# A pooling shift row computed in column tiles, a narrower band, and modulation rows paced anew with a third buffer

## The chip, the cores and the metric

The kernel runs on one core of a Trainium2 chip. The metric is the device time of one execution in microseconds, the median of three runs. Beside the runs there is one profiled execution, from which all rows of the trace come. Engines are named as the profile names them: PE is TensorE (PEld its weight loads), DVE VectorE, ACT ScalarE, POOL GpSimd, SP SyncE, which issues most of the transfers. A name with a q behind it (SPq, ACTq) is the engine's queue of transfers.

## What is computed

Two small transformer stacks in sequence over one sequence of 256 tokens and 1024 features, in float32. The first stack is an mLSTM and sparse-attention layer and then a gated recurrent layer (HGRN2). The second has two layers, each of a mixer and an MLP, both modulated by a vector computed from a conditioning input `c`:

```python
def modulate(h, shift, scale):
    return h * (1.0 + scale[:, None, :]) + shift[:, None, :]

c_act = jax.nn.silu(c)
for i in range(DEPTH):                       # DEPTH = 2
    mod = c_act @ ada_w[i] + ada_b[i]        # 1024 x 6144 weights for each layer
    sh1, sc1, g1, sh2, sc2, g2 = jnp.split(mod, 6, axis=-1)
    h = modulate(rmsnorm(x, norm_mix_g[i]), sh1, sc1)
    y = pool_mixer(h, ...) if i == 0 else sgu_mixer(h, ...)
    x = x + g1[:, None, :] * y
    h = modulate(rmsnorm(x, norm_mlp_g[i]), sh2, sc2)
    x = x + g2[:, None, :] * sq_relu_mlp(h, mlp_w1[i], mlp_w2[i])
return rmsnorm(x, final_g)
```

`pool_mixer` splits the features into four groups of 256. In each it takes the mean over the last 2, 4, 8 or 16 tokens less the token itself, and multiplies by a 256 x 256 matrix. `sq_relu_mlp` is `square(relu(h @ w1)) @ w2` with 4096 hidden features.

## The kernel before, in words

Activations lie transposed, features on the 128 partitions and 256 tokens on the free axis, in eight tiles `xT[:, k, :]`. A float32 product is made of three products in a reduced float32 format: both operands are split into a high and a low part (`hi`, `lo`), and high-high, low-high and high-low are summed (lines 216 to 223). Weights come in pieces of 128 x 1024 (512 KB), two to a load of 1 MB (`load_raw`, line 150; three buffers `raw`). ScalarE copies a piece to `whi` and VectorE subtracts it into `wlo` (lines 155 to 163; four buffers each). The first product of an MLP has 32 tiles of 24 matmuls, one piece each; the second has 8 output tiles of 4 pieces with 16 matmuls each (lines 1002 to 1049).

**Modulation.** The generator `ada` (line 338) computes the two vectors `mod` of 48 columns. For each of 96 chunks it loads 128 x 1024 weights (512 KB, tile `araw`, two buffers, line 350), and VectorE multiplies them with the row `crow` and sums along the row into one column (line 351). This is no work for TensorE. The generator pauses after every one or two chunks; 6 pauses make 8 chunks. `step(upto)` (line 360) runs it to its next pause, as far as `upto` sixths have not been reached, and `finish(upto)` (line 367) runs it up to there. Calls of `step` are spread over all layers: in the first layers up to 30 steps, then one before every second tile of the first MLP's first product (line 1011), one before every second piece of its second (line 1030), one before each tile of the gated layer until 66 steps are done (line 1079), and then one before every fourth tile of the second MLP's first product (line 1013).

**Order.** The order of instructions on each engine is fixed when the program is built, by a list scheduler that goes by the written order as a priority, takes what is ready, and lowers the priority of what `step` issues a little (line 364). What is written late can therefore stand early, if buffers and engine are free. At run time each engine keeps this order, SP's queue of transfers too.

**Pooling** (`pool_layer`, line 960) multiplies by the matrix first, then by a band matrix that does the moving means. Tiles: `z` holds the products by token, `band` the four band matrices, each as 256 columns for the first 128 tokens and 128 columns for the rest. A band entry is nonzero only up to 16 tokens behind. The modulation's shift goes through the matrix by itself: for each of four groups two matmuls in full float32 (line 977) take the shift column, repeated over 128 columns, as the stationary operand, so that the result `row` is the same on all partitions; ScalarE copies it from PSUM (line 978). Then come the transposes that give the norm's reciprocal as a column (`norm.column`, line 299), the 48 pooling matmuls (lines 989 to 991), the eviction with column and row (line 993), and for each of eight feature tiles two band matmuls (lines 998 and 999), the scaled addition to `xT` (line 330), and the next norm's operand (lines 280 and 281) and square (lines 286 to 294).

**The recurrent layer** (`hgrn_layer`, line 786) runs before it: gates and queries, the levels of the recurrence as many small matmuls (line 858), then for two groups of four heads the value columns (`iv_cols`, line 842) and `values` (line 912), and the output projection.

Of the kernel before, what the change touches and what calls it, by code (L numbers as in the profile page):

```python
# [8 lines left out]
F32 = mybir.dt.float32  # L9
# [56 lines left out]
def tile_kernel(ctx: ExitStack, tc: tile.TileContext, io: dict, out: bass.AP):  # L66
    nc = tc.nc
# [270 lines left out]
    def ada(crow):  # L338

        for layer in range(2):
            mod, gains = mods[layer]
            for i in range(6):
                for n in ((0, 1), (2,), (3,), (4, 5), (6,), (7,)):
                    for c in (i * 8 + j for j in n):
                        raw = mk(wpool, [128, 1024], F32, "araw", bufs=2)
                        nc.sync.dma_start(raw, io["ada_w"][layer, c])  # L350
                        V.tensor_tensor_reduce(raw, raw, crow, 1.0, P("ada_b", layer * 48 + c), ALU.mult, ALU.add, mod[:, c : c + 1])  # L351
                    if n == (7,) and i in (1, 4):
                        m, g = i // 3, ("mix_g", "mlp_g")[i // 3]
                        V.scalar_tensor_tensor(gains[:, m * 8 : m * 8 + 8], mod[:, i * 8 : i * 8 + 8], 1.0, P(g, layer * 8, 8), op0=ALU.add, op1=ALU.mult)
                    yield

    side = []
    done = [0]

# [31 lines left out]
    def even_layer(norm, nxt, w):  # L391
        with ExitStack() as es:
# [102 lines left out]

            th = mk(wpool, [128, 1024], F32, "araw", bufs=2)
            tanh(th, crow, scale=0.5)
# [287 lines left out]

    def hgrn_layer(norm, nxt):
        with ExitStack() as es:
# [160 lines left out]
            for _ in levels(4, ATs[1]):  # L948
                next(rest, None)
            tab[0] = Table(EXP_LN, tab[0])  # L950
            for h0 in (0, 4):
                iv_cols(h0)
                values(h0, ATs[h0 // 4])
# [5 lines left out]

    def pool_layer(band, mod, norm, nxt):  # L960


        with ExitStack() as es:
            pp = es.enter_context(tc.tile_pool(name="pp", bufs=1))
            w = Weights(lambda c: io["pool_w"])
            ws = [w.piece(i, 256) for i in range(2)]
            raw = w.raw[0].rearrange("p (k n) -> p k n", n=256)
            gate = mk(pp, [128, 8], F32, "pgate")
            V.tensor_tensor(gate, mod[:, 16:24], P("pool_s"), op=ALU.mult)
            row = mk(pp, [128, 1024], F32, "prow")  # L970
            z = mk(pp, [128, 2, 1024], F32, "pz")
            for g in range(4):
                cs = slice(g * 256, g * 256 + 256)
                ps = mbank()[:, :256]
                for i in range(2):
                    k = 2 * g + i
                    PE.matmul(ps, mod[:, k : k + 1].to_broadcast([128, 128]), raw[:, k, :], start=i == 0, stop=i == 1)
                S.copy(row[:, cs], ps)
            rcol = norm.column()
# [15 lines left out]
            for n in range(8):  # L995
                m = band[:, n // 2, :]
                ps = mbank()[:, :T]
                PE.matmul(ps, z[:, 0, n * 128 : n * 128 + 128], m[:, 0:256], start=True, stop=False)
                PE.matmul(ps[:, 128:256], z[:, 1, n * 128 : n * 128 + 128], m[:, 256:384], start=False, stop=True)
                add(n, ps)  # L1000

    def mlp(layer, mod, norm, nxt):
        with ExitStack() as es:
# [5 lines left out]
            for n in range(32):  # L1009
                if layer == 0 and n % 2 == 0:  # L1010
                    step(11)
                if layer and n % 4 == 3:
                    step(12)
                if layer == 0 and n == 16:
                    sgu_prepare(*consts)
                ps = gbank()[:, : pair.w]
                tile_T(ps, w1, n, pair)
                r = norm.scaled(ps)
                b = mk(tmp, [128, 1], F32, "nb", bufs=3)
                V.tensor_copy(b, ps[:, T : T + 1])  # L1020
                S.activation(r, r, AF.Relu, bias=b)  # L1021
                S.activation(r, r, AF.Square)  # L1022
                split(g[:, n, 0, :], g[:, n, 1, :], r)
            for n in range(8):
# [3 lines left out]
                for c in range(4):  # L1028
                    if layer == 0 and c % 2 == 0:
                        step(11)  # L1030
                    wh, wl = w2.piece(4 * n + c, 128)
# [37 lines left out]
    def sgu_layer(consts, mod, gains, norm, nxt):  # L1069
        with ExitStack() as es:  # L1070
# [7 lines left out]
            def gelu_tile(dst, n):  # L1078
                step(11)
                ps = gbank()[:, : norm.pair.w]  # L1080
                tile_T(ps, w, n, norm.pair)
                t = norm.scaled(ps)
                b = mk(tmp, [128, 1], F32, "nb", bufs=3)
                V.tensor_copy(b, ps[:, T : T + 1])
                tab[0].activation(dst, t, AF.Gelu, bias=b)
# [38 lines left out]
            finish(11)  # L1124
            out_proj(io["sgu_w_out"], y, scaled_add(mod[:, 16:24], nxt))

# [19 lines left out]
    with ExitStack() as es:  # L1146
        bp = es.enter_context(tc.tile_pool(name="bp", bufs=1))
        band = mk(bp, [128, 4, 384], F32, "band")
        nc.sync.dma_start(band, CS2.of(io["cs2"], "band").rearrange("p (g n) -> p g n", g=4))
        norm = Norm(gains[:, 0:8])  # L1150
        hgrn_layer(n1, norm)
        finish(5)
        mid = Norm(gains[:, 8:16], mod[:, 24:32])
        pool_layer(band, mod, norm, mid)
    consts = sgu_consts(ctx.enter_context(tc.tile_pool(name="sc", bufs=1)))
# [190 lines left out]
```

## Time and profile before

| | before |
|---|---|
| median of 3 runs | 828.85 us |
| the runs | 828.87, 828.85, 823.77 us |
| the profiled execution | 830.03 us |
| its span from first to last instruction | 828.2 us |
| mean granted TensorE clock | 0.992 of full speed |
| transfers | 184.64 MB, mean 223 GB/s |

A time in a row is counted from the start of the span. The stages lie roughly so: first layer to 205 us, recurrent layer to 352 us, pooling to 374 us, the first MLP's first product to 464 us, its second product to 558 us, the gated layer to 636 us, the second MLP to 820 us. Matmuls are pipelined: a row's duration is longer than the distance to the next start, and TensorE's busy share says little about its pace; the number of matmuls in a stretch says more. "x" behind a busy time is the number of instructions that touch the stretch.

### The profile page before, as it was taken

The page shows a single profiled execution, that of the slowest core. Times are in us where ns is not written, and L with a number is a line of the kernel's source. Part 1 is how long each engine was busy: PE and PEld are TensorE (multiplying, and loading weights), DVE is VectorE, ACT ScalarE, POOL GpSimd, SP SyncE. Part 2 cuts the span into 40 slices and gives each one's busy share as a digit, 9 for nine tenths or more (in the row PEclk, how much of TensorE's full clock was granted, in tenths as well). Part 3 has the DMA queues.
Part 4 walks back from the last instruction along what each step waited for, and adds up shares of the span by engine and source line. Part 5 has one row for each costly group of instructions (what it writes and reads, how often), then busy time and mean ns, then how long its engine had stood idle before and what let it go on. Part 6 is the DMA issues. An engine that isn't in the chain of part 4 may idle for free.

```text
span 828.2 us, 16357 instructions
## 1 busy us (share of the span) xinstructions
PE 807.2 (97%) x6534; PEld 740.2 (89%) x6534; DVE 672.1 (81%) x1257; ACT 520.3 (63%) x934; POOL 4.9 (1%) x19
## 2 busy tenths in 40 slices
PE   8999999989999999999999999999999999999995
PEld 8968977879999987999999888889999999988884
DVE  7689988899899989999999888876679777755552
ACT  7556765676876556658776734446657777754441
POOL 0000000001000000000000000000000000000000
PEclk9999999999999999999999999999999999999998
DMA  9644566657885777568878889874445454555521
GB/s 345 254 168 144 185 224 221 236 198 251 293 290 204 249 255 258 203 231 271 293 278 285 287 314 316 310 265 154 160 146 204 153 203 163 195 187 175 198 102 51
DMA packets 34635, 184.64 MB, mean 223 GB/s; under 512 B 3968, under 2 KB 4608, under 8 KB 19200
## 3 DMA queue, kind: packets, MB, share of 16 engines
q1 hardware_dynamic: 33696, 181.96, 62.8%
q10 hardware_dynamic: 864, 1.65, 0.6%
q8 instruction: 51, 0.84, 0.4%
q14 instruction: 24, 0.20, 0.1%
HBM read 182.55 MB, written 1.05 MB: 222 GB/s over the span
## 4 chain that ended last, share of the span: by engine, by line
PE 66%; DMA 13%; DVE 12%; ACT 5%; issue 4%; DVEq 0%; ACTq 0%; SPq 0%
PE g L221 12%; PE g L222 12%; DMA araw<-in_ada_w_dram 12%; PE g L223 12%; PE g L1035 9%; PE g L1036 5%; DVE wlo L162 4%; DVE araw L351 3%; ACT whi L161 2%; PE g L207 1%; PE g L208 1%; PE g L206 1%; PE m L858 1%; PE m L748 1%; PE long L776 1%
## 5 line engine op out<-in xcount | busy, mean ns | idle before, releaser
L221 PE MATMUL g<-ahi,whi 128*128 128x258 f32 (+1 forms) x1256 | 360.1, 289 | 4.0 <-ACT ahi L213 2.5
L222 PE MATMUL g<-alo,whi 128*128 128x258 f32 (+1 forms) x1256 | 357.6, 286 | 0.1
L223 PE MATMUL g<-ahi,wlo 128*128 128x258 f32 (+1 forms) x1256 | 356.6, 285 | 0.0
L162 DVE TENSOR_TENSOR wlo<-raw,whi 128x1024 fp32r<-128x1024 f32 (+1 forms) x238 | 288.6, 1216 | 73.5 <-ACT whi L161 72.9
L161 ACT CAST whi<-raw 128x1024 fp32r<-128x1024 f32 (+1 forms) x238 | 246.2, 1043 | 160.1 <-PE g L222 68.0
L221 PEld LDWEIGHTS g<-ahi,whi 128*128 128x128 f32 x1256 | 238.7, 191 | 8.7 <-ACT ahi L213 3.1
L222 PEld LDWEIGHTS g<-alo,whi 128*128 128x128 f32 x1256 | 240.2, 191 | 2.1 <-issue 0.8
L223 PEld LDWEIGHTS g<-ahi,wlo 128*128 128x128 f32 x1256 | 239.3, 191 | 1.7 <-issue 1.0
L1035 PE MATMUL g<-ghl,whi 128*128 128x512 f32 x512 | 179.9, 394 | 0.6 <-DVE nb L1020 0.6
L1036 PE MATMUL g<-ghl,wlo 128*128 128x256 f32 x512 | 143.5, 280 | 2.7 <-DVE wlo L162 2.4
L351 DVE CUSTOM_DVE_ANT_0 araw<-araw,row_c,prm 128x1024 f32<-128x1024 f32 x96 | 122.5, 1279 | 23.5 <-DMA araw<-in_ada_w_dram 23.3
L1035 PEld LDWEIGHTS g<-ghl,whi 128*128 128x128 f32 x512 | 96.0, 187 | 23.3 <-issue 0.7
L1036 PEld LDWEIGHTS g<-ghl,wlo 128*128 128x128 f32 x512 | 96.0, 187 | 4.0 <-DVE wlo L162 3.9
L310 DVE TENSOR_TENSOR nt<-g,nrstd 128x256 f32<-128x256 f32 x133 | 55.5, 419 | 17.3 <-PE g L223 16.9
L1021 ACT ACTIVATE nt<-nt,nb 128x256 f32<-128x256 f32 x64 | 32.4, 507 | 21.3 <-DVE nb L1020 21.3
L280 ACT ACTIVATE ahi<-xT,gains 128x256 fp32r<-128x256 f32 x32 | 16.2, 507 | 36.2 <-DVE xT L330 32.3
L214 DVE TENSOR_TENSOR ghl<-nt,ghl 128x256 fp32r<-128x256 f32 x64 | 27.0, 423 | 3.8 <-ACT ghl L213 1.4
L1022 ACT ACTIVATE nt<-nt 128x256 f32<-128x256 f32 x64 | 26.7, 418 | 1.9
L213 ACT CAST ghl<-nt 128x256 fp32r<-128x256 f32 x64 | 25.9, 406 | 1.9
L208 PE MATMUL g<-wlo,ahi 128*128 128x512 f32 (+1 forms) x64 | 24.3, 379 | 0.0
L206 PE MATMUL g<-whi,ahi 128*128 128x512 f32 (+1 forms) x64 | 24.2, 378 | 0.0
L286 ACT ACTIVATE sq<-xT 128x256 f32<-128x256 f32 x56 | 22.3, 405 | 3.0 <-DVE xT L330 3.0
(290 smaller groups left out, 758.7 us busy)
## 6 DMA issues: line engine op xcount, KB each, us to landing
raw<-in_mlp_w_dram SPq DMA_DIRECT2D x64, 1024.0 KB, 5.0
araw<-in_ada_w_dram SPq DMA_DIRECT2D x96, 512.0 KB, 5.1
raw<-in_ev_w_in_dram SPq DMA_DIRECT2D x17, 1024.0 KB, 6.1
raw<-in_od_w_in_dram SPq DMA_DIRECT2D x16, 1024.0 KB, 6.0
raw<-in_sgu_w_in_dram SPq DMA_DIRECT2D x8, 1024.0 KB, 4.7
raw<-in_ev_w_out_dram SPq DMA_DIRECT2D x4, 1024.0 KB, 4.9
raw<-in_od_w_out_dram SPq DMA_DIRECT2D x4, 1024.0 KB, 4.9
raw<-in_sgu_w_out_dram SPq DMA_DIRECT2D x4, 1024.0 KB, 4.7
```

What stands on the lines that cost most here:

```text
L161: S.copy(hi[:, c], r[:, c])
L162: V.tensor_sub(lo[:, c], r[:, c], hi[:, c])
L206: PE.matmul(ps[tb], pair.hi(k)[:, ts_], wh[:, j, :], start=st, stop=False)
L208: PE.matmul(ps[tb], pair.hi(k)[:, ts_], wl[:, j, :], start=False, stop=sp)
L221: PE.matmul(ps, wh(k), ah(k), start=st, stop=False)
L222: PE.matmul(ps, wh(k), al(k), start=False, stop=False)
L223: PE.matmul(ps, wl(k), ah(k), start=False, stop=sp)
L310: V.tensor_tensor(t, ps[:, :T], self.r, op=ALU.mult)
L351: V.tensor_tensor_reduce(raw, raw, crow, 1.0, P("ada_b", layer * 48 + c), ALU.mult, ALU.add, mod[:, c : c + 1])
L1021: S.activation(r, r, AF.Relu, bias=b)
L1035: PE.matmul(ps, wh[:, k, :], a.rearrange("p s t -> p (s t)"), start=st, stop=sp, skip_group_check=True)
L1036: PE.matmul(ps[:, :T], wl[:, k, :], a[:, 0, :], start=False, stop=sp, skip_group_check=True)
```

## The change

The shift row is computed by a new function `pool_row` inside the recurrent layer, between the levels and the value columns. Each of its eight matmuls has 32 stationary columns and writes 32 partitions of one PSUM tile, each group in its own column tile (`tile_position`). One ScalarE copy takes the tile to `row4`, and four transfers on ScalarE's queue spread one partition of each group over the 128 partitions of `row`. The pooling weights are loaded for it once more. In the band the first matmul covers 144 columns instead of 256. `araw` gets a third buffer. The calls of `step` in the MLPs and in the gated layer become `pace(tiles)`, which counts units (8 for a tile or a piece) and steps the generator along a table: 30 to 36 steps over the first MLP's first product, 36 to 60 over its second, 60 to 66 over the gated layer's tiles, 66 to 72 over the second MLP's first product.

```diff
-                        raw = mk(wpool, [128, 1024], F32, "araw", bufs=2)
+                        raw = mk(wpool, [128, 1024], F32, "araw", bufs=3)
...
-    done = [0]
+
+    done = [0, 0]
+    PACE = ((0, 30), (256, 36), (512, 60), (640, 66), (704, 66), (960, 72))
+
+    def pace(tiles):
+
+        u = done[1]
+        done[1] += tiles
+        for (u0, s0), (u1, s1) in zip(PACE, PACE[1:]):
+            if u0 <= u < u1:
+                while done[0] * (u1 - u0) < s0 * (u1 - u0) + (s1 - s0) * (u - u0):
+                    step(12)
...
-    def hgrn_layer(norm, nxt):
+    def hgrn_layer(norm, nxt, between):
...
             tab[0] = Table(EXP_LN, tab[0])
+            between()
             for h0 in (0, 4):
                 iv_cols(h0)
...
+    def pool_row(row4, row, mod):
+
+        raw = load_raw(io["pool_w"]).rearrange("p (k n) -> p k n", n=256)
+        ps = mbank()[:, :256]
+        for i in range(2):
+            for g in range(4):
+                k = 2 * g + i
+                PE.matmul(ps[32 * g : 32 * g + 32], mod[:, k : k + 1].to_broadcast([128, 32]), raw[:, k, :], start=i == 0, stop=i == 1, tile_position=(0, 32 * g))
+        S.copy(row4, ps)
+        for g in range(4):
+            nc.scalar.dma_start(row[:, g * 256 : g * 256 + 256], row4[32 * g : 32 * g + 1, None, :].to_broadcast([1, 128, 256]))
...
-            raw = w.raw[0].rearrange("p (k n) -> p k n", n=256)
...
-            row = mk(pp, [128, 1024], F32, "prow")
             z = mk(pp, [128, 2, 1024], F32, "pz")
-            for g in range(4):
-                cs = slice(g * 256, g * 256 + 256)
-                ps = mbank()[:, :256]
-                for i in range(2):
-                    k = 2 * g + i
-                    PE.matmul(ps, mod[:, k : k + 1].to_broadcast([128, 128]), raw[:, k, :], start=i == 0, stop=i == 1)
-                S.copy(row[:, cs], ps)
...
-                PE.matmul(ps, z[:, 0, n * 128 : n * 128 + 128], m[:, 0:256], start=True, stop=False)
-                PE.matmul(ps[:, 128:256], z[:, 1, n * 128 : n * 128 + 128], m[:, 256:384], start=False, stop=True)
+
+                PE.matmul(ps[:, 0:144], z[:, 0, n * 128 : n * 128 + 128], m[:, 0:144], start=True, stop=False, skip_group_check=True)
+                PE.matmul(ps[:, 128:256], z[:, 1, n * 128 : n * 128 + 128], m[:, 256:384], start=False, stop=True, skip_group_check=True)
...
-                if layer == 0 and n % 2 == 0:
-                    step(11)
-                if layer and n % 4 == 3:
-                    step(12)
+                pace(8)
...
-                    if layer == 0 and c % 2 == 0:
-                        step(11)
+                    pace(8)
...
-                step(11)
+                pace(8)
...
-            out_proj(io["sgu_w_out"], y, scaled_add(mod[:, 16:24], nxt))
+            out_proj(io["sgu_w_out"], y, scaled_add(mod[:, 16:24], nxt), every=0)
+            pace(64)
...
+        row4, row = mk(bp, [128, 256], F32, "prow4"), mk(bp, [128, 1024], F32, "prow")
         norm = Norm(gains[:, 0:8])
-        hgrn_layer(n1, norm)
+        hgrn_layer(n1, norm, lambda: pool_row(row4, row, mod))
```

## Rows read from the trace of the kernel before

**Rows 1.** The page, part 1: busy us, share of the span, instructions of each engine.

```profile
PE 807.2 (97%) x6534; PEld 740.2 (89%) x6534; DVE 672.1 (81%) x1257; ACT 520.3 (63%) x934; POOL 4.9 (1%) x19
```

**Rows 2.** Table by stage: stretch, length, each engine's busy us, granted clock, DMA share, GB/s.

```profile
300.00:352.00 52.00, 52.00 (x319) 45.00 (x318) 48.02 (x87) 32.58 (x57) 0.00 (x0) 1.00 0.71 252
352.00:374.00 22.00, 21.80 (x150) 20.05 (x149) 20.76 (x46) 12.02 (x29) 0.00 (x0) 1.00 0.69 236
440.00:460.00 20.00, 20.00 (x167) 19.86 (x166) 18.02 (x37) 14.99 (x27) 0.00 (x0) 1.00 0.86 292
500.00:520.00 20.00, 19.02 (x109) 16.37 (x108) 17.03 (x27) 6.46 (x10) 0.00 (x0) 1.00 0.90 316
520.00:540.00 20.00, 18.56 (x106) 15.92 (x105) 16.47 (x23) 9.95 (x14) 0.00 (x0) 1.00 0.89 314
660.00:680.00 20.00, 20.00 (x168) 20.00 (x167) 14.88 (x28) 15.79 (x29) 0.00 (x0) 1.00 0.49 163
```

**Rows 3.** Line 1035 in each MLP: duration min/median/max ns, first and last start.

```profile
L1035 PE MATMUL g<-ghl,whi x256: 389/394/477, 464.1 to 557.9; 128*128 128x512 f32 x128
...
L1035 PE MATMUL g<-ghl,whi x256: 389/392/583, 728.5 to 818.3; 128*128 128x512 f32 x128
```

**Rows 4.** Table by stage for line 351 alone, two records for each chunk.

```profile
374.00:465.00 91.00, 26.09 (x41) 1.00 0.82 285
465.00:541.60 76.60, 25.86 (x42) 1.00 0.88 308
541.60:829.00 287.40, 0.00 (x0) 0.99 0.48 166
```

**Rows 5.** Waits over the whole span: us in total, times, longest.

```profile
DVE araw L351 <- DMA araw<-in_ada_w_dram: 23.3, 22, 2.8
...
DVE pz L993 <- PE g L991: 1.2, 2, 0.6
```

**Rows 6.** Timeline of VectorE and TensorE around 530 us: start, duration, idle before in brackets.

```profile
528.27 1.28 DVE L351 CUSTOM_DVE_ANT_0 araw<-araw,row_c,prm 128x1024 f32<-128x1024 f32 x1 [2.80 <-DMA araw<-in_ada_w_dram]
...
529.60 1.28 DVE L351 CUSTOM_DVE_ANT_0 araw<-araw,row_c,prm 128x1024 f32<-128x1024 f32 x1
...
531.21 1.22 DVE L162 TENSOR_TENSOR wlo<-raw,whi 128x1024 fp32r<-128x1024 f32 x1
...
532.48 0.39 PE L1036 MATMUL g<-ghl,wlo 128*128 128x256 f32 x1 [1.44 <-DVE wlo L162]
```

**Rows 7.** The page, part 6: issues, KB of each, median us to landing.

```profile
raw<-in_mlp_w_dram SPq DMA_DIRECT2D x64, 1024.0 KB, 5.0
araw<-in_ada_w_dram SPq DMA_DIRECT2D x96, 512.0 KB, 5.1
```

**Rows 8.** Timeline of pooling, TensorE and at the end VectorE.

```profile
352.97 1.89 PE L977 MATMUL m<-raw,mod 128*128 128x256 f32 x8
...
356.93 0.36 PE L989 MATMUL g<-whi,ahi 128*128 128x256 f32 x1
...
362.69 0.59 PE L998 MATMUL m<-band,pz 128*128 128x256 f32 x2
363.12 0.38 PE L999 MATMUL m<-band,pz 128*128 128x128 f32 x2
363.34 0.60 PE L998 MATMUL m<-band,pz 128*128 128x256 f32 x2
...
377.65 0.37 PE L221 MATMUL g<-ahi,whi 128*128 128x258 f32 x1
...
377.02 0.42 DVE L310 TENSOR_TENSOR nt<-g,nrstd 128x256 f32<-128x256 f32 x1
```

**Rows 9.** Timelines: column-tiled matmuls in the first layer, and an issue on ScalarE's queue.

```profile
43.19 1.08 PE L643 MATMUL m<-raw,cX 128*32 128x128 f32 x32
...
372.69 0.44 ACTq L1055 DMA_DIRECT2D ws<-in_sgu_w_s_dram  x1
```

**Rows 10.** TensorE's timeline and the table by stage where its clock fell.

```profile
185.91 0.50 PE L221 MATMUL g<-ahi,whi 128*128 128x256 f32 x2 [1.68 <-ACT ahi L213]
...
188.00:190.00 2.00, 2.00 (x12) 2.00 (x11) 1.97 (x7) 0.48 (x2) 0.00 (x0) 0.50 0.19 61
```

More of the change, by code (lines that the diff above doesn't have):

```diff
@@ L494, in even_layer @@
             tab[0] = Table(EXP_TANH, tab[0])
-            th = mk(wpool, [128, 1024], F32, "araw", bufs=2)
+            th = mk(wpool, [128, 1024], F32, "araw", bufs=3)
             tanh(th, crow, scale=0.5)
@@ L955, in hgrn_layer, with pool_layer @@
             out_proj(io["od_w_out"], y, add_x(nxt), 5, 1)
-    def pool_layer(band, mod, norm, nxt):
+    def pool_row(row4, row, mod):
[8 more added lines that the diff above has]
+            nc.scalar.dma_start(row[:, g * 256 : g * 256 + 256], row4[32 * g : 32 * g + 1, None, :].to_broadcast([1, 128, 256]))
+    def pool_layer(row, band, mod, norm, nxt):
         with ExitStack() as es:
@@ L1149, in tile_kernel @@
         nc.sync.dma_start(band, CS2.of(io["cs2"], "band").rearrange("p (g n) -> p g n", g=4))
+        row4, row = mk(bp, [128, 256], F32, "prow4"), mk(bp, [128, 1024], F32, "prow")
         norm = Norm(gains[:, 0:8])
-        hgrn_layer(n1, norm)
+        hgrn_layer(n1, norm, lambda: pool_row(row4, row, mod))
         finish(5)
         mid = Norm(gains[:, 8:16], mod[:, 24:32])
-        pool_layer(band, mod, norm, mid)
+        pool_layer(row, band, mod, norm, mid)
     consts = sgu_consts(ctx.enter_context(tc.tile_pool(name="sc", bufs=1)))
```

## The prediction

> **What bounds the kernel now.** I began with the part of the page that gives each engine's busy share: TensorE is busy for 97% of the span, VectorE for 81% [rows 1]. So little can be gained by making another engine faster, and the places where TensorE lags its own best pace must be found. The busy share cannot show them, since matmuls overlap in the record, so I went to the table by stage and counted matmuls instead [rows 2]. In the second MLP's first product 168 matmuls start in 20 us, a pace of 0.119 us each, and the granted clock is full. In the first MLP's first product the pace is the same within a record or so (167), but VectorE is already busy 18.0 of 20 us. In the first MLP's second product only 109 and 106 records stand in 20 us.
>
> Next I compared the two MLPs' second products, which are the same work: from first to last matmul start 93.8 us in the first, 89.8 us in the second [rows 3]. The difference, 4.0 us, is what the modulation costs there, because the second MLP has none beside it: 41 records (two for each chunk) run in the first product, 42 in the second, none after 557 us [rows 4]. The waits say how [rows 5, 6]: VectorE waited 23.3 us in 22 waits for a modulation row to land. The longest one (2.80 us, at 528 us) is followed by two chunks back to back, then by the weight split, and TensorE stands still 1.44 us for that split. The data is late because the DMA engines are full: 314 to 316 GB/s at a share of 0.89 to 0.90 [rows 2]. One piece of weights is 512 KB, one chunk is 512 KB [rows 7]. The second product has 32 pieces in 89.8 us, 2.81 us each. 21 chunks ran between 465 and 541.6 us, 27 pieces, or 0.78 a piece; that is 0.933 MB a piece, and at 315 GB/s it takes 2.96 us, 0.15 us too long, times 27 is 4.1 us. That meets the 4.0 us measured, so here the bound is the transfer rate.
>
> The pooling stage (352 to 377 us) is bound otherwise. VectorE is busy 20.8 of 22 us [rows 2] and TensorE has no gap either, but part of what TensorE does is filling: the shift row's 16 passes (a row shows eight, 0.23 us from start to start, so 3.6 us in all) run while the norm's last column and square are on their way, and push the 48 pooling matmuls back to 356.93 us [rows 8]. VectorE waits for these, twice 0.6 us [rows 5].
>
> **The change, part by part.** *The shift row.* It leaves the pooling stage: 3.6 us of TensorE and four ScalarE copies. TensorE can then start pooling matmuls at 352 us; the PSUM tiles let three of the four groups finish before the norm is there. VectorE then finds three groups done when the reciprocal column arrives. So its two waits go (1.2 us), and the norm's exponential and its transposes no longer stand behind a copy and the passes (I estimate 1 us, from the order in [rows 8]). What follows on VectorE, eight scaled additions with their operand and square work, stays. From below the gain is 0 (VectorE was the bound and still is), from above the whole 3.6 us and the band's 1.5 us. I take 2.3 us, nearest to VectorE's row, since what sets the resumption at 377.65 us [rows 8] is VectorE's first eviction at 377.02 us.
>
> *The band.* The first matmul of each pair goes from 256 to 144 columns: its two passes start 0.43 us before the next matmul, the pair takes 0.65 us [rows 8], so 112 columns of 256 less save 0.19 us, eight times 1.5 us. But from the first of these matmuls at 362.69 us to the next product's first eviction at 377.02 us VectorE, which is nearly full, takes 14.3 us for the eight tiles, 1.8 us each, so TensorE's saving is hidden; I take 0 beyond the 2.3 us. If that cover were gone it would be 1.5 us.
>
> *The row in the recurrent layer.* It returns there: eight matmuls on 32 output rows each, in four column tiles. The nearest row is the compression's: 32 records of 128 columns on 32-row tiles within 1.08 us [rows 9]; 16 records of 256 columns make about 1.0 us. If the tiles did not run side by side it would be the old 3.6 us. TensorE is full in that stretch (52.0 of 52 us [rows 2]), so it counts. ScalarE gains one copy and four issues at 0.44 us [rows 9], some 2.2 us; weight copies stand behind them, and the cover is that it is busy 32.6 of 52 us there. On SP's queue the 1 MB load of the pooling weights is put ahead of the value weights and takes one of three raw buffers. With the 0.5 MB spread it is 1.5 MB where the DMA share is 0.71: at 350 GB/s 4.5 us out of 15 us free. I take +0.8 us, bounds 0 and +3.6.
>
> *Pacing and the third buffer.* As written, 6 steps (8 chunks) fall into the first product instead of 16 (21), and 24 steps (32 chunks) into the second instead of 16 (21). But the order in which an engine gets its work is not the written one. By 465 us the old text has written 46 steps, 61 chunks; 96 less 21, that is 75, have run. All 96 are done by 541.6 us, though ten steps are written later, in the gated layer and the second MLP [rows 4, 7]. The chunks run ahead as far as buffers and VectorE's gaps let them. So I expect the new places to matter little and the buffer to matter: three rows in flight instead of two. Some three more chunks will be done before the first MLP, some 24 instead of 21 in its first product, and about 15 will be left for the second, at up to one a piece. With one a piece the stage needs 1.049 MB in 2.81 us, 373 GB/s, and does not get it. The 316 GB/s came at a share of 0.90, so with deeper queues up to 351 may come. At 335, an estimate between the two, a piece takes 3.13 us, 0.32 us too long, times 15 is 4.8 us, against 4.0 us before. In the first product, 377.65 to 464.1 us is 86.4 us for 29 tiles that would take 82.9 at 0.119 us a matmul; part of the 3.5 us is the gated layer's preparation, written inside that loop. I take 1.3 us as VectorE's waits on rows that the buffer removes. Sum: -0.5 us. Bounds: all of the loss goes (4.0 and 1.3 us, -5.3), or the written pace holds (below, +11.1).
>
> The Trainium skill, "DMA: Bandwidth & Descriptors", section Specifications, gives a core about 358 GB/s from HBM as its limit. By that figure a piece with one chunk takes 2.93 us, an estimate from the page: 15 such pieces lose 1.8 us, where the sum above loses 4.8. The rate in these rows stayed below it at 314 to 316.
>
> *Sum.* -2.3 + 0.8 - 0.5 = -2.0 us. The profiled execution took 830.03 us (its span 828.2), 1.2 us above the median of 828.85. Against that execution it makes 828.0, and carried over to the median 826.9; I give 827.
>
> **Rivals.** (1) *The new pace holds* and 32 chunks fall into the second product, one a piece. For it: the text says so, and a lower rank could hold chunks back. Against it: how far they run ahead in [rows 4]. At 316 GB/s the product takes 32 x 3.32 = 106.2 us, 12.4 more than 93.8; less 1.3 for an unloaded first product and 1.5 for pooling with the row, +9.6: 838 us. At 351 it takes 95.6, 1.8 more, and the sum is -1.0: 828. It ends slower by over 1% from 320 GB/s down.
>
> (2) *The buffer removes the whole loss*: rows are there in time, and the chunks spread thinly enough. For it: the 23.3 us of waits, each for one transfer. Against it: the DMA share of 0.9. -5.3, and pooling with the row at up to -3.5: 820 us.
>
> (3) *Nothing comes of it*: VectorE bounds pooling as before, and the chunks that are done early load the DMA engines denser in exchange: 829 us. For it: VectorE's 20.8 of 22 us.
>
> (4) *TensorE falls idle in pooling*, as its filling is gone, and its clock drops. Before, after an idle time of 1.68 us the granted clock stood at 0.50, the 1.2 GHz level, in a stretch two microseconds later [rows 10]. At half rate for some 3 us it costs 1.5 us: 828.5 us. Against it: the 48 matmuls and three tiles of the MLP fill the time nearly to the end.
>
> **How the numbers follow.** The forecast (823 to 830 by its own bounds) has 0.45, rival 1 has 0.17, rival 2 has 0.20, rivals 3 and 4 together 0.18. Differences of up to 1% (8.3 us) are about what a measurement of this kernel tells from no change. Faster by over 1% means below 820.6: most of rival 2, 0.18. Slower by over 1%, above 837.1, is most of rival 1 and some unforeseen disorder in the fixed orders of the earlier layers: 0.14. Within 1%: 0.68. The range from 818 to 837 leaves out the outer ends of rivals 1 and 2, about 0.2.
>
> **What would show it.** Pooling: its matmuls start near 352 us instead of 357 and the first free-running MLP tile 2 us earlier after the same last output projection; if that distance is still 26 us, VectorE was all of it. Row: 16 passes in about 1 us before 310 us; in 3.6 us if the tiles do not run side by side. Modulation: chunks counted by stretch; the last one near 500 us if the buffer decides, near 690 us (in the second MLP) if the pace does. Second product: 93.8 us before; about 94 or 95 by the sum, 90 by rival 2, 106 by rival 1, with GB/s in it at 335, under 300, or 316. The prediction is wrong if chunks stay where they are written, or if a stretch before 300 us changes by over 2 us.

## The result and the profile after

| | before | after |
|---|---|---|
| median of the timed runs beside each other | 828.85 us (7 runs) | 833.7 us (7 runs, 832.86 to 837.31) |
| ratio after to before | | 1.008, 95% interval 1.0057 to 1.0103 |
| span of the profiled execution | 828.2 us | 831.5 us |
| mean granted clock | 0.992 | 0.985 |

The change makes the kernel slower by 0.8%, 4.7 to 8.5 us (the ratio is taken over all runs, so it is not the quotient of the two medians). That lies within 1% of before, where the forecast put 0.68, but on the other side of zero: the predicted 827.0 was 2 us below before.

The engines' totals hardly tell it. This is the page of after, part 1, in the columns of [rows 1]:

```profile
PE 802.7 (97%) x6534; PEld 735.9 (88%) x6534; DVE 670.6 (81%) x1257; ACT 520.9 (63%) x931; POOL 4.9 (1%) x19
```

The table by stage does. It is the view of [rows 2], of after:

```profile
300.00:352.00 52.00, 46.42 (x245) 37.92 (x244) 40.63 (x71) 25.68 (x44) 0.00 (x0) 0.93 0.81 257
352.00:374.00 22.00, 20.52 (x168) 19.92 (x167) 21.68 (x45) 12.70 (x26) 0.00 (x0) 1.00 0.75 263
...
480.00:500.00 20.00, 20.00 (x117) 17.45 (x116) 14.97 (x22) 9.39 (x14) 0.00 (x0) 1.00 0.89 331
500.00:520.00 20.00, 20.00 (x116) 17.45 (x116) 19.11 (x29) 8.87 (x12) 0.00 (x0) 1.00 0.82 311
520.00:540.00 20.00, 20.00 (x116) 17.45 (x115) 15.17 (x20) 9.16 (x13) 0.00 (x0) 1.00 0.71 257
```

Between 300 and 352 us TensorE started 319 matmuls before [rows 2] and 245 now; it is busy 46.42 of 52 us, at a mean clock of 0.93, and VectorE and ScalarE are each busy about 7 us less. From 500 to 540 us the opposite: 116 matmuls in each 20 us where 109 and 106 stood.

To place the difference I cut every trace at the same landmarks (first and last start of a line): first level matmul, last level matmul, last value matmul (line 919 of before, 930 of after), last band matmul, first and last matmul of the first MLP's second product. The lengths between them, in us; where a kernel was profiled more than once, each trace has its number:

| stage ends at | before (3 traces) | after (2 traces) | what after's part of it is |
|---|---|---|---|
| first level matmul | 236.4, 237.8, 236.3 | 237.6, 239.8 | first layer: +1.9 |
| last level matmul | 62.8, 62.4, 62.4 | 62.9, 62.8 | +0.3 |
| last value matmul | 28.7, 28.6, 28.7 | 38.3, 38.5 | value stage: +9.7 |
| last band matmul | 41.0, 40.6, 40.6 | 39.0, 39.1 | out projection and pooling: -1.7 |
| second product, first | 95.2, 94.8, 96.9 | 92.7, 93.6 | first product: -2.5 |
| second product, last | 93.8, 94.4, 94.1 | 90.0, 89.9 | second product: -4.2 |
| end | 270.3, 270.8, 270.4 | 271.0, 270.5 | +0.3 |

One stage lost 9.7 us, the rest together gained about 6.

**Inside the value stage.** Four rows of ScalarE and its queue, two of VectorE and two of TensorE, from after's timeline (start, duration, engine, line; in brackets the idle time before and who ended it):

```profile
299.00 3.86 ACTq L982 DMA_DIRECT2D prow<-prow  x3
302.90 0.59 ACT L908 COPY hAT<-m 128x512 f32<-128x512 f32 x1 [3.53 <-PE g L208]
302.94 5.07 ACTq L982 DMA_DIRECT2D prow<-prow  x1
308.11 3.89 ACT L161 CAST whi<-raw 128x1024 fp32r<-128x1024 f32 x4 [3.32 <-PE g L208]
...
309.19 3.50 DVE L162 TENSOR_TENSOR wlo<-raw,whi 128x1024 fp32r<-128x1024 f32 x3 [5.13 <-ACT whi L161]
316.69 1.28 DVE L351 CUSTOM_DVE_ANT_0 araw<-araw,row_c,prm 128x1024 f32<-128x1024 f32 x1 [3.35 <-DMA araw<-in_ada_w_dram]
...
313.50 1.71 PE L930 MATMUL m<-hAT,hiv 128*128 128x256 f32 x6 [2.50 <-DVE hiv L857]
318.70 1.65 PE L931 MATMUL m<-hAT,hiv 128*128 128x128 f32 x6 [2.22 <-DVE hiv L857]
```

The four spread transfers held ScalarE's queue for 3.86 us (three of them) and 5.07 us (the fourth). Behind them stands the weight copy at 308.11 (its bracket names TensorE, but it starts 0.1 us after the last issue ends at 308.01); VectorE's split waited 5.13 us for it. Then VectorE waits 3.35 us for a modulation row, TensorE twice for VectorE (2.50 and 2.22 us), and its granted clock falls to 0.50, the 1.2 GHz level. The stretches of 4 us of after, and below them two of before (columns as in [rows 2]):

```profile
304.00:308.00 4.00, 4.00 (x19) 3.25 (x18) 0.06 (x2) 0.79 (x1) 0.00 (x0) 1.00 0.87 101
308.00:312.00 4.00, 3.00 (x13) 2.07 (x12) 2.81 (x3) 3.89 (x4) 0.00 (x0) 1.00 0.93 259
312.00:316.00 4.00, 2.50 (x9) 2.00 (x9) 1.35 (x2) 0.00 (x1) 0.00 (x0) 0.84 0.93 225
316.00:320.00 4.00, 1.78 (x8) 1.30 (x7) 3.13 (x5) 0.42 (x2) 0.00 (x0) 0.50 0.64 154
320.00:324.00 4.00, 4.00 (x16) 2.66 (x15) 1.78 (x4) 2.29 (x5) 0.00 (x0) 0.81 0.99 391
```

```profile
304.00:308.00 4.00, 4.00 (x19) 3.24 (x18) 3.20 (x5) 1.05 (x1) 0.00 (x0) 1.00 0.96 334
316.00:320.00 4.00, 4.00 (x19) 3.25 (x18) 4.00 (x9) 2.94 (x5) 0.00 (x0) 1.00 0.55 173
```

The telling pair is the last two numbers of 304 to 308 us. Before, the DMA engines were busy 0.96 and moved 334 GB/s; after, 0.87 and 101 GB/s. They are nearly as busy and move less than a third. Who takes their time stands in the list of queues of after from 302 to 306 us (queue, packets, MB, share of the 16 engines):

```profile
q10 hardware_dynamic: 160, 0.15, 53.8%
q1 hardware_dynamic: 93, 0.62, 38.9%
```

q10 is ScalarE's queue, the spread: 0.15 MB took 53.8% of the engines' time, while the weights on q1 got 0.62 MB through in 38.9%. The loads beside it are late for that: a pair of output-projection pieces lands after 8.9 us, a spread transfer after 13.5 (medians); below them the pair before:

```profile
raw<-in_od_w_out_dram SPq DMA_DIRECT2D x4, 1024.0 KB, 8.9
...
prow<-prow ACTq DMA_DIRECT2D x4, 128.0 KB, 13.5
```

```profile
raw<-in_od_w_out_dram SPq DMA_DIRECT2D x4, 1024.0 KB, 4.9
```

### The profile page after: what moved, and what is told of

It is laid out like the page before. It is cut to its first block, busy times and chain, and to the rows that moved or that the text cites. A ratio compares the mean times of both kernels' runs of the same rounds, so it can differ in the third digit from the quotient of the medians.

```text
span 831.5 us, 16358 instructions
## 1 busy us (share of the span) xinstructions
PE 802.7 (97%) x6534; PEld 735.9 (88%) x6534; DVE 670.6 (81%) x1257; ACT 520.9 (63%) x931; POOL 4.9 (1%) x19
## 4 chain that ended last, share of the span: by engine, by line
PE 86%; DVE 4%; DMA 3%; ACT 3%; issue 2%; ACTq 1%; DVEq 0%; SPq 0%
PE g L221 17%; PE g L223 17%; PE g L222 17%; PE g L1047 14%; PE g L1048 7%; PE m L869 1%; PE m L759 1%; DVE wlo L162 1%; DMA araw<-in_ada_w_dram 1%; PE long L787 1%; ACT whi L161 1%; PE m L294 1%; DMA raw<-in_od_w_in_dram 1%; PE m L780 1%; DMA raw<-in_ev_w_in_dram 1%
## 5 line engine op out<-in xcount | busy, mean ns | idle before, releaser
L223 PEld LDWEIGHTS g<-ahi,wlo 128*128 128x128 f32 x1256 | 237.8, 190 | 4.2 <-DVE wlo L162 2.5
L207 PE MATMUL g<-whi,alo 128*128 128x512 f32 (+1 forms) x64 | 24.6, 384 | 0.0
```

What stands on the lines that cost most here:

```text
L223: PE.matmul(ps, wl(k), ah(k), start=False, stop=sp)
```

## The experiments

My theory after this reading: the spread, which reads one partition for each group, costs the 9.7 us, and the third buffer gives what the MLP gained. Rivals: the row's new place or the second load of the pooling weights; ScalarE standing in its issues; transfers of 1 KB pieces as such; the pace instead of the buffer; a loss in the second product that belongs to single executions. Ratios are to before's runs on the same chip, with 95% intervals.

**Without column tiles and spread (direct).**

```diff
...
-                PE.matmul(ps[32 * g : 32 * g + 32], mod[:, k : k + 1].to_broadcast([128, 32]), ...)
-        S.copy(row4, ps)
-        for g in range(4):
-            nc.scalar.dma_start(row[:, g * 256 : g * 256 + 256], row4[32 * g : 32 * g + 1, None, :]...)
+                PE.matmul(ps, mod[:, k : k + 1].to_broadcast([128, 128]), raw[:, k, :], ...)
+            S.copy(row[:, g * 256 : g * 256 + 256], ps)
```

> The changed kernel, but the shift row is computed in the recurrent layer as before was: eight matmuls with 128 stationary columns, four ScalarE copies, no column tiles and no spread transfers. Theory (the four spread transfers cost the 9.6 us lost in the value stage): that loss goes, 16 passes of 0.23 us (3.6 us) stand in place of 1.0 us, so 833.7 - 9.6 + 2.6 = 826.7 us, and the last value matmul starts near 332 us instead of 338.8. Rival 1 (moving the row with its second load of the pooling weights costs it, however the row is spread): the loss stays, 833 to 836 us, value stage ends near 339 to 341.

Measured: 829.51 us, ratio 1.0029 (1.0009 to 1.005). Value stage 32.2 us: 6.2 less than after, and 3.5 more than before, the price of the 16 passes. The place and the second load cost nothing that shows in this stage. The total is 2.8 us above the expected; no run here shows why.

**The spread on GpSimd's queue (spread_pool).**

```diff
-            nc.scalar.dma_start(row[:, g * 256 : g * 256 + 256], row4[32 * g : 32 * g + 1, None, :]...)
+            nc.gpsimd.dma_start(row[:, g * 256 : g * 256 + 256], row4[32 * g : 32 * g + 1, None, :]...)
```

> The changed kernel with the four spread transfers issued by GpSimd's queue instead of ScalarE's. If ScalarE standing in its own issues (3.9 and 5.1 us in the records) is the whole cost, the loss of 9.6 us goes: about 824 us. If the one-partition transfers hold up the other transfers (the loads of weights and modulation rows), it stays: about 833 us, with VectorE waits of 2 to 3 us on modulation rows near 304 to 323 us. My theory has both parts, the issue the larger one: 827 to 829 us.

Measured: 839.33 us, ratio 1.0152 (1.0128 to 1.0175), worse than after; value stage 41.1 us. Its wait for a modulation row and its queue of the spread, both from 296 to 345 us, and the stretch from 316 to 320 us:

```profile
DVE araw L351 <- DMA araw<-in_ada_w_dram: 9.5, 1, 9.5
```

```profile
q0 software_dynamic: 192, 0.52, 20.2%
```

```profile
316.00:320.00 4.00, 0.00 (x0) 0.00 (x0) 0.00 (x0) 0.00 (x0) 0.00 (x0) 0.57 0.83 244
```

ScalarE is free of the issues here, and VectorE still waits 9.5 us for one modulation row, with no engine at work for 4 us. So the loss does not need ScalarE standing in its issues: the held DMA engines are enough for it. I had given the issue the larger part; that was wrong. From this queue the spread holds the engines for longer than from ScalarE's (20.2 against 15.1% of their time in these 49 us, shown below), so the run does not say how much of after's 9.7 us the issues added. The Trainium skill ("DMA: Bandwidth & Descriptors", Rules for kernel authors) says that issuing from another engine saves issue time only, since all queues share the 16 engines; the trace agrees (12.4 us lost against before, where ScalarE's queue lost 9.7).

**Plain copies of 1 KB from 128 partitions (direct_copy).** The edit against direct:

```diff
...
-            S.copy(row[:, g * 256 : g * 256 + 256], ps)
+            S.copy((row0 if g < 3 else row)[:, g * 256 : g * 256 + 256], ps)
+        for g in range(3):
+            nc.scalar.dma_start(row[:, g * 256 : g * 256 + 256], row0[:, g * 256 : g * 256 + 256])
```

> The kernel with the row computed directly (829.5 us), with three of its four groups taken through an extra tile and moved into place by three plain transfers on ScalarE's queue: 128 partitions to 128 partitions, 1 KB each, 384 packets (the spread has 512 of 1 KB, read from one partition a group). If the price lies in reading one partition, these three cost next to nothing: 829 to 831 us, value stage 32 to 33 us. If it lies in transfers of 1 KB pieces from tile to tile, three quarters of the 6.1 us come back: 833 to 835 us, value stage near 37 us.

Measured: 830.02 us, ratio 1.003 (1.0001 to 1.0059), value stage 33.1 us, 0.9 more than direct. ScalarE's queue from 296 to 345 us, first of after, then of direct_copy, and one of direct_copy's three issues:

```profile
q10 hardware_dynamic: 576, 0.52, 15.1%
```

```profile
q10 hardware_dynamic: 432, 0.39, 2.4%
```

```profile
300.82 0.52 ACTq L982 DMA_DIRECT2D prow<-prow  x1
```

0.39 MB in the same 1 KB pieces cost 2.4% of the engines' time in this stretch; the spread's 0.52 MB cost 15.1% of it in after. By 1 KB that is 0.024 x 16 x 49 us / 384 = 0.05 us of an engine against 0.151 x 16 x 49 / 512 = 0.23. The size of the pieces is not what is dear; reading one partition is. The issues take 0.5 us, as forecast.

**The spread through DRAM (dram_hop, row_hop).**

```diff
-        for g in range(4):
-            nc.scalar.dma_start(row[:, ...], row4[32 * g : 32 * g + 1, None, :].to_broadcast([1, 128, 256]))
+        nc.gpsimd.dma_start(hop, row4[0:128:32, :])
+        nc.gpsimd.dma_start(row, <hop as one row of 1024>.to_broadcast([128, 1024]))
...
```

> The changed kernel with the row's spread led through DRAM on GpSimd's queue: one transfer writes the four rows (4 KB), a second reads them back into all 128 partitions, 4 KB each. The 512 KB written into the tile are the same; their source is not one partition. Theory (the one-partition read holds up the DMA engines): value stage 29.7 to 31 us instead of 38.3, 833.7 - 8 = 826 us. If any transfer of 512 KB at this place costs it: 832 to 834 us. With a waiting GpSimd queue as the cost: also above 830.

Measured: 827.63 us, ratio 0.9994 (0.9972 to 1.0017): level with before. Value stage 30.1 us. The queue of the two transfers, 296 to 345 us:

```profile
q0 software_dynamic: 176, 0.53, 2.7%
```

The same 512 KB reach the same tile from the same queue as in spread_pool at 2.7 instead of 20.2% of the engines' time, and about 7 us of the kernel come back (0.9994 against 1.008), close to what the theory expected (826 us, value stage 29.7 to 31). Between these two kernels only the way of the bytes differs, and pieces of 1 KB are not dear by themselves (direct_copy); so the dear part is the read of one partition.

The row part alone, on the kernel before, with the spread as in the change (row_only) and through DRAM (row_hop):

> The kernel before with the row part alone (column tiles, spread by ScalarE's queue, load moved); modulation, two buffers and band as before. Theory: +9.6 in the value stage, -2.6 in pooling, 828.9 + 7.0 = 835.9 us. By the forecast's terms for this part (-2.3 + 0.8): 827.4 us. If the loss in the value stage came from the third buffer's earlier modulation loads instead (a rival), also near 826 to 828 us.

> The kernel before with the row part alone (column tiles, load moved), its spread led through DRAM on GpSimd's queue; two buffers, old steps, old band. With the spread from one partition on ScalarE's queue the same kernel took 838.3 us. Theory (nothing but the source of the spread was dear): value stage 30.1 us (+1.4), pooling as in that kernel 37.8 us (-3.2): 827.8 - 1.8 = 826.0 us. If the row's place itself cost time beside the spread: 829 us or more.

Measured: row_only 838.27 us, ratio 1.0124 (1.0082 to 1.0165); row_hop 830.0 us, ratio 1.0021 (0.9995 to 1.0047). Value stage 38.5 and 31.1 us, pooling 37.8 us in both (-2.9 to before). The loss is the row part's, not that of the buffer or the pace. row_only loses more than after: beside +9.8 us in the value stage and -2.9 in pooling its second product is 98.2 us long, 4.1 more than before. row_hop missed its 826.0 and lies where its expectation put a cost of the place itself (829 us or more): its value stage is 2.4 us longer than before, of which the 16 passes explain 1.1, and its second product takes 95.6 us. That the row with a cheap spread is faster than before is not shown: value stage and pooling together gain 0.5 us in the traces, by the timed runs it is level or 0.5% slower.

**Buffer and pace.**

```diff
 (buf3)          araw: bufs=2 -> bufs=3, nothing else
 (late3)         araw: a third buffer only for every third chunk from chunk 36 on
 (pace)          the new done, PACE and pace() with all their calls; bufs=2
 (no_late_rows)  the loads of chunks 76 to 96 left out
 (hop_buf2)      the changed kernel, spread through DRAM, bufs=2
```

> The kernel before with a third buffer for the modulation rows and nothing else. Theory (the buffer alone gives what the MLP gained, 1.6 us in the first product and 3.8 us in the second): 828.9 - 5.4 = 823.5 us, last second-product matmul 5 us earlier. Rival (the new pacing gives it): 828 to 829 us, second product still 93 to 94 us long.

> The kernel before with the third modulation buffer only for every third chunk from chunk 36 on (after the first layer), so that the first layer's order stays that of before. The kernel with the buffer everywhere had its first level matmul at 239.1 us instead of 236.4 and an MLP 5.8 us shorter, yet 828.95 us. Theory (the buffer helps the MLP and disturbs the first layer): 2.5 us less, 826.4 us. Rival (before's MLP loss was that one execution's): 828 us or more, no gain over before.

> The kernel before with the new pacing of the steps alone; two buffers. If the pace gives what the first MLP gained in the profile (rival): second product 90 us, 823 to 824 us. If the written places matter little, as forecast: second product 93 to 95 us, 827 to 829 us. If the pace as written held: 106 us in the second product, 838 us.

> The kernel before without the loads of the last 21 modulation chunks (from the 76th on, those that run in the second product); VectorE's 21 instructions stay, on data that is there, and give a wrong modulation of the second layer. If the second product's 4 us over its free length are lost in every execution: 827.8 - 4 = 823.8 us timed, 89.9 us in the profile. If they are lost only where the profile is taken (its executions of before took 830.0 and 831.2 us, the median is 827.8): 89.9 us in the profile, a profiled time near 826 us, and timed 827 to 828 us, no gain.

> The changed kernel with the spread led through DRAM and two modulation buffers instead of three (827.6 us with three). By the profiles the third buffer costs 2.5 us in the first layer and gives 5.8 us in the first MLP: without it 830 to 831 us. By the timed runs of the buffer alone (828.95 against 827.5) it gives nothing: 826 to 827 us without it, though the profile shows 93 to 95 us in the second product.

| | timed, us | ratio | first layer | pooling | first product | second product |
|---|---|---|---|---|---|---|
| buf3 (2 traces) | 828.95 | 1.0022 (1.0005 to 1.0039) | 239.1, 238.1 | 42.3, 42.3 | 93.3, 93.3 | 89.9, 89.9 |
| late3 | 827.97 | 0.9993 (0.997 to 1.0016) | 239.4 | 40.6 | 93.6 | 89.9 |
| pace (2 traces) | 827.26 | 0.9984 (0.9961 to 1.0008) | 235.7, 235.1 | 40.6, 40.5 | 94.3, 94.1 | 90.4, 91.7 |
| no_late_rows | 825.77 | 0.9982 (0.9959 to 1.0005) | 236.4 | 40.6 | 94.1 | 89.9 |
| hop_buf2 | 830.68 | 1.0019 (0.9991 to 1.0048) | 234.5 | 37.6 | 93.9 | 97.0 |

Three things follow. *First*, every trace with a third buffer has its second product at 89.9 to 90.0 us; with two, and with all rows loaded, it goes from 90.4 to 98.2 us (row_only). Without the late loads, though VectorE still does their chunks' work there, it is 89.9 us (no_late_rows), so the loads are what lengthens it. With the third buffer fewer chunks are left for it: 17 in after and 14 in buf3, where before has 21. But the pace with two buffers has 90.4 and 91.7, with as many records in it as before: its modulation instructions from 462 to 552 us and, below, TensorE in 470 to 530 us:

```profile
462.00:552.00 90.00, 26.29 (x42) 1.00 0.87 312
```

```profile
470.00:530.00 60.00, 60.00 (x342) 51.95 (x341) 51.69 (x73) 27.12 (x38) 0.00 (x0) 1.00 0.91 328
```

42 records, as before [rows 4], at 312 GB/s over its 90 us, and no gap in the 60 us where they run at 328. So before was not bound by the rate there: the same transfers fit into 90 us if they come at other moments. What before loses there is TensorE's wait for the weight split. The page, part 5, gives it for the low part's weight loads of both second products (busy time and mean, then the idle time before them and who ended most of it), of before, pace and after:

```profile
L1036 PEld LDWEIGHTS g<-ghl,wlo 128*128 128x128 f32 x512 | 96.0, 187 | 4.0 <-DVE wlo L162 3.9
```

```profile
L1042 PEld LDWEIGHTS g<-ghl,wlo 128*128 128x128 f32 x512 | 96.0, 187 | 0.6 <-DVE wlo L162 0.5
```

```profile
L1048 PEld LDWEIGHTS g<-ghl,wlo 128*128 128x128 f32 x512 | 96.1, 188 | 0.1
```

In the other traces of before this idle time is 4.8 and 4.0 us, in pace's second one 2.1: it meets what each of these products takes beyond 89.8 us within 0.3 us. The three kernels with the row and two buffers (row_only, row_hop, hop_buf2) differ: 23 chunks run in their second product, and TensorE's weight loads wait there once 2.9 to 4.9 us for VectorE's square of the norm (line 289 of before). Why they wait there stays open.

*Second*, the third buffer costs time in the first layer. The stretch from 100 to 120 us of before and of buf3, and 112 to 118 us of buf3:

```profile
100.00:120.00 20.00, 20.00 (x141) 16.70 (x140) 18.02 (x44) 12.25 (x38) 0.00 (x0) 1.00 0.55 188
```

```profile
100.00:120.00 20.00, 18.66 (x109) 14.59 (x108) 16.62 (x43) 10.34 (x32) 0.00 (x0) 0.83 0.60 194
...
112.00:118.00 6.00, 5.18 (x24) 4.14 (x24) 4.12 (x11) 2.05 (x6) 0.00 (x0) 0.50 0.79 272
```

I read this as a changed order: with a third buffer other instructions are ready when the fixed orders are made. TensorE gets gaps (0.52 us for ScalarE's `w` at 110.7, 0.82 us at 114.0), and from 112 to 118 us its clock is 0.50, the 1.2 GHz level. All nine traces with three buffers (late3 counted) have the first level matmul at 237.6 to 240.2 us, all nine with two at 234.5 to 237.8. Late3 was to avoid it, and has 239.4: its order changed later in the layer (100 matmuls in 180 to 200 us, 138 before). The attempt failed: no gain, where 2.5 us were expected.

*Third*, the gains of the traces are not found in the timed runs. The buffer alone shortens the traced execution by 2 to 4 us and is 0.05 to 0.39% slower in the timed runs. To see whether the traces were chance I took further ones:

> The kernel before once more, unchanged, for a second profile. Its first profiled execution took 830.03 us, 2.6 us above the median of the 23 runs by now (827.48). If the loss in the first MLP's second product (93.8 us where 89.9 would do) belongs to that execution more than to the kernel, this one shows 90 to 92 us there and a span of 824 to 826 us, and the third buffer had little to win. If it is the kernel's, 93 to 94 us again and a span near 828 us.

> The kernel before, a third profile. If the second product's length varies by execution with two buffers: anything from 90 to 95 us, and the run's time moves with it. If it belongs to the kernel: 93.8 to 94.4 us as in the first two.

> The changed kernel, a second profile. Value stage 37 to 40 us again if the spread's loss belongs to the kernel (38.3 in the first); second product 90.0 us; first layer 237 to 239 us.

> The third buffer alone, a second profile. If the buffer takes the transfers' loss away in every execution: second product 89.9 us again. If the first layer's 2.7 us more belong to the buffer: first level matmul near 239 us again, otherwise 236 to 237.

> The new pace alone with two buffers, a second profile. If the pace shortens the second product by itself: 90 to 91 us again (90.4 in the first). If that was the execution: 92 to 95 us.

Measured: the stage lengths come back within 1 or 2 us (both tables above). They belong to the kernels, and the expectation that the second product varies from execution to execution fell. But the profiled executions of before took 830.0, 831.2 and 831.1 us, 2.2 to 3.4 us above the median of its timed runs (827.8 us), those of pace 824.2 and 825.2, 2 to 3 us below theirs (827.26), those of buf3 828.0 and 827.0, 1 to 2 below. Single runs of before scatter by more than that: of the 35 timed beside pace, from 823.1 to 832.9 us, nine took 830 us or more. So this may be chance; what else would set a profiled execution apart stays open. The timed runs bound what the second product's transfers can cost in all: no_late_rows, which has none of them, is 0.18% faster, at most 0.41%, 3.4 us; its trace would make it 6 us. Its 825.77 us lie between the two cases of its expectation.

With the new row the buffer looks better: 827.63 us with it (dram_hop), 830.68 without (hop_buf2), as the profiles had let expect (830 to 831), though the intervals of the two ratios overlap. No version that does the whole work beat before by more than the measurement is uncertain; the pace alone came nearest.

## Why the prediction was wrong, step by step

**The row in the recurrent layer: wrong.** This is the failed step, and the one that made the kernel slower: +0.8 us, with bounds 0 and +3.6, measured +9.7 us in the traces. TensorE's term was right: 16 records in 1.07 us, as estimated from the column tiles of [rows 9]:

```profile
297.46 1.07 PE L979 MATMUL m<-raw,mod 128*32 128x256 f32 x16
```

Wrong were both terms of the spread. "Four issues at 0.44 us" took 8.9 us: the row behind 0.44 is a transfer between DRAM and 128 partitions. And "1.5 MB at 350 GB/s, 4.5 us out of 15 free" counted bytes. Of the 0.52 MB of the spread only 0.15 MB went through in 4 us (37 GB/s), and they took half of the engines' time meanwhile. A price by bytes was taken from weight loads, and nothing in the trace of before read one partition many times; the upper bound should have said that no row bounds this. With the cover gone (weights, modulation rows and ScalarE's copies all late at once), 4.7 us of waits on TensorE followed, and some 7 us at the 1.2 GHz level (from the means 0.84, 0.50 and 0.81 of the three stretches from 312 to 324 us).

**Pooling: right.** The forecast -2.3 meets -1.7 in after's stage, and -2.9 where the row part stands alone. From the last value matmul to the first pooling matmul it is 29.0 us before and 23.5 after, and to the first free-running tile of the MLP 49.8 and 46.9: the two signs that the prediction named. VectorE's two waits of 0.6 us shrank to one of 0.3; it remains the bound, busy 22.0 of 23 us (362 to 385 us). The third buffer costs pooling some 1.3 to 1.6 us of this (after 39.1 against 37.8 with two; buf3 42.3 against 40.7): ten modulation records run between 352 and 374 us in buf3, five before.

**Band at 0: not contradicted.** hop_buf2 (144 columns) has 37.6 us for pooling, row_hop (256 columns) 37.8; they differ in the pace too, and the band was not run by itself.

**Rival 4 (TensorE idle in pooling): seen, without a price.** One gap of 1.65 us in its weight loads, while VectorE is busy 2.00 of 2 us (368 to 370 us), and the clock stayed at 1.00:

```profile
369.43 0.54 PEld L1014 LDWEIGHTS m<-band,pz 128*128 128x128 f32 x4 [1.65 <-issue]
```

**Pacing and the third buffer: the cause of the loss misread.** In the traces the two products gain 2.5 and 4.2 us, more than the bound of 5.3, where the sum had -0.5; the timed runs do not show this gain, so the size of the term stays open. The mechanism is rival 2's, by its own signs: 90 us in the second product at under 300 GB/s, measured 90.0 us at 282. Modulation records in after by stretch, columns as in [rows 4]:

```profile
374.00:470.00 96.00, 26.97 (x42) 1.00 0.81 286
470.00:530.00 60.00, 21.55 (x33) 1.00 0.85 318
530.00:832.00 302.00, 0.36 (x2) 0.99 0.48 165
```

Rival 1 is refuted: the written places do not hold, some 17 chunks run in the second product instead of 32, the last ends at 530 us, neither near 500 nor near 690. In the first product 21 chunks run, not the 24 I expected. The step that failed here, the second one, is "here the bound is the transfer rate", from which 4.8 us followed: the second product needs [rows 3] 90 us of matmuls, and 331 GB/s pass in it without a gap (480 to 500 us above), 328 in the pace's with two buffers. That the 4.1 us worked out from the rate met the measured 4.0 was luck. What cost before its 4 us was when a row landed, while VectorE stood in its wait and the weight split behind it [rows 6]: TensorE's waits for that split make 3.9 us in all. It was named in the prediction and then put down to a full pipe. Of the 23.3 us of waits that rival 2 counted, 12.0 lie in the second product.

```profile
L1047 PE MATMUL g<-ghl,whi x256: 390/393/399, 470.5 to 560.5; 128*128 128x512 f32 x128
...
L1047 PE MATMUL g<-ghl,whi x256: 389/393/586, 731.0 to 820.9; 128*128 128x512 f32 x128
```

The two second products of after are now equally long, 90.0 and 89.9 us; in [rows 3] they were not.

**The first layer: not in the prediction's sum.** +1.9 us from the third buffer, as I read it by a changed order and the clock. The text named a change of over 2 us before 300 us as a sign of being wrong; it came near that.

Together: +1.9 + 0.3 + 9.7 - 1.7 - 2.5 - 4.2 + 0.3 = +3.8 us between the mean traces (832.9 less 829.0); the timed runs say +6.6 (4.7 to 8.5). Most of the difference lies in the traced executions themselves: before's took 2.2 to 3.4 us more than its median of 827.8, after's 0.4 less and 2.3 more than its own. That the kernel still came out at 833.7, inside the stated 818 to 837, is luck as far as the traces go: +9.7 us in the value stage, where the sum had +0.8, were offset in part by 6.7 us gained in the first MLP's products, where it had 0.5.

## What to carry to other kernels

Price a transfer by the time it takes of the DMA engines, not by its bytes: a tile filled from one partition took five times the engine time of the same bytes read from DRAM or from 128 partitions, and everything queued beside it was late. Before a wait is put down to a full pipe, look for the same transfers running in another stretch or kernel without it. A buffer more can change the fixed orders upstream of the place it is meant for, so read the stages ahead of it too, and check a gain of a few us that a trace shows against the timed runs.

## What the runs showed of the hardware

Reading one SBUF partition 128 times in 1 KB pieces cost 0.23 us of a DMA engine for each (0.31 from GpSimd's queue: 0.202 x 16 x 49 / 512); the same pieces from 128 partitions 0.05, and DRAM rows of 4 KB 0.04 for each KB (0.027 x 16 x 49 / 512). The issuing queue stood up to 5.07 us in one issue while the engines were held, where the same queue took 0.5 us for a plain copy. The Trainium skill ("DMA: Bandwidth & Descriptors", Why small descriptors are slow (HBM only)) says that transfers from tile to tile don't suffer from small pieces; direct_copy agrees for its 1 KB pieces (0.05 us each), and the spread has pieces of the same size, so its price is another one, that of the single source partition.
